# Mixture of experts: three experts in f32r and five in float32 column tiles, where six and two stood

## The chip, the cores and the metric

The program runs on one core of a Trainium2 chip. The metric is the time of one execution on the device, in microseconds (us); the lower the better. One profiled execution gives the trace.

## What is computed

The reference is a two-layer block of a diffusion transformer on 256 latent and 256 context tokens of width 1024. Layer 0 mixes by Hyena convolutions and attention and has a dense feed-forward part, layer 1 mixes by an S5 scan and has a mixture of eight experts, of which each latent token takes two. Only the mixture of experts is touched:

```python
logits = (t @ router).astype(F32)                 # t: 256 x 1024
top_val, top_idx = lax.top_k(logits, TOP_K)       # TOP_K = 2 of 8
top_w = jax.nn.softmax(top_val, axis=-1)
gates = jnp.sum(jax.nn.one_hot(top_idx, N_EXPERTS, dtype=F32) * top_w[..., None], axis=1)
for e in range(N_EXPERTS):
    he = jax.nn.silu(t @ w_gate[e]) * (t @ w_up[e])   # 1024 x 3584 each
    out = out + gates[:, e:e + 1].astype(t.dtype) * (he @ w_down[e])   # 3584 x 1024
```

## The kernel before

The layers before the mixture take up the first half of the span and stay as they are. Then the router's logits are ranked per token (`route_tile`), which gives each chosen token its place in the expert's list (`posm`) and the number of tokens of each expert (`cnt`). An expert computes only the tokens that chose it: a matrix `Sel` of ones and zeros (places against tokens) gathers them with matmuls (`gather`), and its transpose scatters the results back into `acc` (`scatter`).

**Slots.** Experts 0 and 1 have the slots 0 and 1. `route_order` sorts the other six by count; the slots 2 to 7 get their numbers as registers of SP (`nc.values_load`), so the loads of these experts' weights (`eload`) are issued at an address that SP reads only then. Slots 0 to 5 have 128 places each. The last two, `PAIR` and `PAIR + 1`, have 64 places each and share one tile of 128.

**Two ways to multiply.** The weights come as tiles of 1 MB (128 x 2048 float32, `kload`, `eload`), from a ring of raw tiles (`w`, `x1w`, `zw`: 8 in the steady part); an expert has 42 of them. Slots 0 to 5 (`up_big`, `down_big`) use f32r: `wsplit` splits each tile into a high and a low part on ACT (L196) and DVE (L197), and `mm3` issues three matmuls (L186 to L188) on each block of 128x512 weights. The pair (`up_pair`, `down_pair`) multiplies the raw tile in float32, with no split: an expert's 64 places are 64 columns of TensorE's array, and the two experts' matmuls write the lower and the upper 64 partitions of the same bank (L1844, L1887).

**Order.** The columns of 3584 are cut into `NP = 4` pieces of 1024, 1024, 1024 and 512. A task is a slot and a piece: its gate and up products, then, one task later, its down product. The tasks of the pair stand at the places 2, 8, 14 and 20 of the list. SP issues the loads in this order; ACT, DVE and PE have their instructions from the recording layer's scheduler, and each engine works its list in order. At the end `finish`, `scatter` and a norm follow. If an expert has more tokens than places, a second path (`overflow_expert`) computes the rest; it stands behind a branch on the largest excess.

Of the kernel before, what the change touches and what calls it, by code (L numbers as in the profile page):

```python
# [17 lines left out]
P = 128  # L18
# [10 lines left out]
def build(tc, A, out, stages=("s0", "mix0", "ffn0", "mix1", "moe"), dbg=None):  # L29
# [1127 lines left out]
    R_, rr = {}, {}  # L1157

# [17 lines left out]
    def route_setup(mp, tp, hf):  # L1176

        hfS = hp.tile([P, 2, 2, D], F32R, tag="hH", name="hfS")
        R_.update(tp=tp, hf=hf, hfH=hfS[:, 0], hfL=hfS[:, 1])
        for nm in ("lg", "rk", "sel", "gate", "posm"):  # L1180
            R_[nm] = mp.tile([P, 2, NE], F32, name=nm)
        R_["cnt"] = mp.tile([P, NE], F32, name="cnt")
        R_["tie"] = mp.tile([P, NE, NE], F32, name="tie")
        S.dma_start(R_["tie"].rearrange("p a b -> p (a b)"), A["k_tie"])

    def route_tile(t, x_):
# [42 lines left out]
        rr[t] = r  # L1229
# [9 lines left out]
    def route_slots(tp, e2):  # L1239

        Sel = tp.tile([P, 2, 2, P], F32R, tag="Sel", name="Sel", bufs=1)
# [5 lines left out]
    def place(t, s):  # L1247
        return R_["posm"][:, t, s:s + 1] if s < 2 else R_["posS"][:, t, s - 2:s - 1]

    def gate_of(t, s):  # L1250
        return R_["gate"][:, t, s:s + 1] if s < 2 else R_["gateS"][:, t, s - 2:s - 1]

    def route_gates(tp, m2):
# [3 lines left out]
        v = [m2.tile([P, 2, 1], F32, name="v%d" % i, bufs=1) for i in range(2)]  # L1257
# [18 lines left out]
    def route_order(tp, m2):  # L1276


        n = NE - 2
        cnt, posm, gate = R_["cnt"], R_["posm"], R_["gate"]  # L1280
        sh = [P, n, n]

        def scr(nm):
            return m2.tile([P, n, n], F32, name="or" + nm, tag="or" + nm, bufs=1)
        a, q = scr("H"), scr("L")
        co = cnt[:, 2:].unsqueeze(1).to_broadcast(sh)
        ce = cnt[:, 2:].unsqueeze(2).to_broadcast(sh)
        V.tensor_tensor(q, co, ce, op=OP.is_equal)
        V.tensor_tensor(a, co, ce, op=OP.is_gt)
        V.tensor_tensor(q, q, R_["tie"][:, 2:, 2:], op=OP.mult)  # L1290
# [13 lines left out]
        R_["gateS"] = tp.tile([P, 2, n], F32, name="gateS")  # L1304
        num = tp.tile([P, n], F32, name="onum")
        numi = tp.tile([P, n], I32, name="onumi")
        by_place(num, iota[:, 1:1 + n])
        V.tensor_copy(numi, num)
        for t in range(2):
            by_place(R_["posS"][:, t, :], posm[:, t, 2:])  # L1310
            by_place(R_["gateS"][:, t, :], gate[:, t, 2:])
        cap = R_["cap"] = tp.tile([P, NE], F32, name="ocap")
        G.memset(cap[:, 0:2], float(P))
        V.tensor_scalar(cap[:, 2:], rank, float(n - 2) - 0.5, -64.0, OP.is_gt, OP.mult)
        V.tensor_scalar(cap[:, 2:], cap[:, 2:], float(P), None, OP.add)
# [3 lines left out]
    def route_scatter(SelT, Sel):  # L1319

        b = fbank("selT")
        for e in range(2):
            for t in range(2):
                o = e * 256 + t * P
                T.transpose(b[:, o:o + P], Sel[:, t, e, :].bitcast(F32), ident)
        S.activation(SelT, b.rearrange("p (e t) -> p e t", e=2), AF.Copy)
# [18 lines left out]
    def moe_first(sp, w0=()):  # L1345
# [6 lines left out]
        ws = [kload(A["od_moe_w_gate"][0, 0], 2 * u, 0, 1024) for u in range(2)]  # L1352
# [291 lines left out]
    def overflow_expert(ei, rnd, op_, hq, m2, dP, hfH, hfL, acc, Wg, Wu, Wd, NC):  # L1644
# [11 lines left out]
        xg = m2.tile([P, KD, 256], F32, tag="xgL", name="xg2", bufs=1)  # L1656
# [41 lines left out]
        y = hq.tile([P, D], F32, tag="hL", name="oy")  # L1698
# [10 lines left out]
    if "moe" in stages:  # L1709
# [27 lines left out]
        if True:  # L1737
            m2 = open_pool(es4, "moe2", 2)

            def gather(e2):  # L1740

                if e2 % 2:
                    xB = hq.tile([P, 2, KD, 256], F32R, tag="hL", name="xB")
                    xH, xL = xB[:, 0], xB[:, 1]
                else:
                    xH = m2.tile([P, KD, 256], F32R, tag="xgH", name="xgH", bufs=1)
                    xL = m2.tile([P, KD, 256], F32R, tag="xgL", name="xgL", bufs=1)
                Sel = route_slots(mp, e2)
                for k2 in range(KD // 2):
                    b = bank("xg", "yb") if e2 == 0 and k2 % 2 else fbank("xg")  # L1750
                    u = hd_tile()
                    for k in range(2):
                        kc = (k2 * 2 + k) * P
                        cs = slice(k * 256, (k + 1) * 256)
                        for i, (src, t) in enumerate(((hfH, 0), (hfH, 1), (hfL, 0), (hfL, 1))):
                            T.matmul(b[:, cs], src[:, t, kc:kc + P], Sel[:, t].rearrange("p e s -> p (e s)"),
                                     start=(i == 0), stop=(i == 3))
                    for k in range(2):
                        cs = slice(k * 256, (k + 1) * 256)
                        modulate(u[:, cs], b[:, cs], k2 * 2 + k, k)  # L1760
                    ks = slice(k2 * 2, k2 * 2 + 2)
                    u = u.rearrange("p (k s) -> p k s", k=2)
                    S.activation(xH[:, ks, :], u, AF.Copy)
                    V.tensor_tensor(xL[:, ks, :], u, xH[:, ks, :].bitcast(F32), op=OP.subtract)
                SelT[e2] = m2.tile([P, 2, 256], F32R, tag="SelT", name="SelT", bufs=2)
                route_scatter(SelT[e2], Sel)
                return xH, xL

            def gather_pair():

                Sel = mp.tile([P, 2, P], F32R, tag="Sel", name="SelP", bufs=1)
                for t in range(2):
                    for i in range(2):
                        V.tensor_scalar(Sel[:, t, 64 * i:64 * i + 64], iota[:, 0:64], place(t, PAIR + i), None,
                                        OP.is_equal)
                xP = m2.tile([P, KD, P], F32, name="xP", bufs=1)
                for k4 in range(2):
                    b = fbank("xp")
                    for k in range(4):
                        kc = (k4 * 4 + k) * P  # L1780
                        for i, (src, t) in enumerate(((hfH, 0), (hfH, 1), (hfL, 0), (hfL, 1))):
                            T.matmul(b[:, k * P:(k + 1) * P], src[:, t, kc:kc + P], Sel[:, t, :],
                                     start=(i == 0), stop=(i == 3))
                    for k in range(4):
                        modulate(xP[:, k4 * 4 + k, :], b[:, k * P:(k + 1) * P], k4 * 4 + k, k % 2)
                b = fbank("selP")
                for t in range(2):
                    T.transpose(b[:, t * P:(t + 1) * P], Sel[:, t, :].bitcast(F32), ident)
                for t in range(2):
                    T.matmul(b[:, 256:258], Sel[:, t, :].bitcast(F32),  # L1790
                             R_["gateS"][:, t, PAIR - 2:PAIR], start=(t == 0), stop=(t == 1))
                SelT[PAIR] = m2.tile([P, 256], F32R, name="SelTP", bufs=1)
                S.activation(SelT[PAIR], b[:, 0:256], AF.Copy)
                gp = m2.tile([P, 1], F32, name="gp", bufs=1)
                V.tensor_copy(gp[0:64], b[0:64, 256:257])
                V.tensor_copy(gp[64:128], b[64:128, 257:258])
                return xP, gp

            NP = 4
# [5 lines left out]
            def hidden(bs):  # L1805

                hds_ = []
                for g, u in zip(*bs):
                    hd = hd_tile()
                    S.activation(hd, g, AF.Silu)  # L1810
                    V.tensor_tensor(hd, u, hd, op=OP.mult)
                    hds_.append(hd)
                return hds_

            def up_big(s, c, xH, xL, so):
                o, w = piece(c)
                nh, nk = w // 512, 2048 // w
                bs = []
                for i, W in enumerate((Wg, Wu)):
                    bb = [bank("mgu", "gu", 4) for _ in range(nh)]  # L1820
                    for u in range(KD // nk):
                        get = first.pop((s, c, i, u), None) or wsplit(eload(W, num[s], nk * u, o, w))
                        for h in range(nh):
                            for kk in range(nk):
                                k = nk * u + kk
                                mm3(bb[h], xH[:, k, so:so + P], xL[:, k, so:so + P],
                                    *get(kk * w + h * 512, 512), k == 0, k == KD - 1)
                    bs.append(bb)
                return hidden(bs)

            def up_pair(c, xP):
                o, w = piece(c)
                nh, nk = w // 512, 2048 // w
                bs = []
                for W in (Wg, Wu):
                    bb = [bank("pgu", "gu", 4) for _ in range(nh)]
                    for u in range(KD // nk):
                        ws = [eload(W, num[PAIR + i], nk * u, o, w) for i in range(2)]
# [250 lines left out]
```

## Time and profile before

| | |
|---|---|
| median of 3 runs | 2019.73 us (2016.52 to 2019.82) |
| the profiled execution | 2018.54 us |
| its span, first to last instruction | 2016.8 us |
| mean granted clock of TensorE | 0.969 |
| PE busy | 1860.4 us (92%) |
| DVE, ACT busy | 1394.2, 1037.2 us |
| DMA queue of the weights (q1) | 514.73 MB, 68.2% of 16 engines |

The page's first part gives each engine's busy time, its second cuts the span into 40 slices. A stretch's own limit is read from tables of stretches (busy time of each engine, granted clock, share and rate of the DMA engines) and from the instructions in order of time. The expert stage runs from about 1041 us to 1997 us.

### The profile page before, as it was taken

The page shows a single profiled execution, that of the slowest core. Times are in us where ns is not written, and L with a number is a line of the kernel's source. Part 1 is how long each engine was busy: PE and PEld are TensorE (multiplying, and loading weights), DVE is VectorE, ACT ScalarE, POOL GpSimd, SP SyncE. Part 2 cuts the span into 40 slices and gives each one's busy share as a digit, 9 for nine tenths or more (in the row PEclk, how much of TensorE's full clock was granted, in tenths as well). Part 3 has the DMA queues.
Part 4 walks back from the last instruction along what each step waited for, and adds up shares of the span by engine and source line. Part 5 has one row for each costly group of instructions (what it writes and reads, how often), then busy time and mean ns, then how long its engine had stood idle before and what let it go on. Part 6 is the DMA issues. An engine that isn't in the chain of part 4 may idle for free. (4 is left out here: it accounts for less than half of the span.)

```text
span 2016.8 us, 25616 instructions
## 1 busy us (share of the span) xinstructions
PE 1860.4 (92%) x9278; PEld 1369.1 (68%) x9278; DVE 1394.2 (69%) x2054; ACT 1037.2 (51%) x1492; POOL 160.2 (8%) x144
## 2 busy tenths in 40 slices
PE   5999999989999999865879999999999999999996
PEld 2667667867777787655658467846785687567775
DVE  6575775688875476486778358935883588578886
ACT  3522355543333365325466347724772477457765
POOL 1000310001111001055220000000000000000000
PEclk9999999989999999887979999999999999999998
DMA  9474314436666656637557999899999999999992
GB/s 350 162 261 149 134 42 176 160 112 212 219 209 201 221 188 245 233 121 272 211 223 261 368 409 397 332 356 410 405 368 378 413 384 360 340 385 352 355 336 109
DMA packets 196970, 545.55 MB, mean 271 GB/s; under 512 B 32620, under 2 KB 62421, under 8 KB 189285
## 3 DMA queue, kind: packets, MB, share of 16 engines
q1 hardware_dynamic: 165884, 514.73, 68.2%
q10 hardware_dynamic: 29400, 23.50, 4.0%
q0 software_dynamic: 1552, 5.62, 1.0%
q8 instruction: 75, 1.23, 0.2%
q14 instruction: 59, 0.48, 0.1%
HBM read 517.85 MB, written 25.89 MB: 270 GB/s over the span
## 5 line engine op out<-in xcount | busy, mean ns | idle before, releaser
L197 DVE TENSOR_TENSOR wl<-w,wh 128x1024 fp32r<-128x1024 f32 x380 | 449.7, 1224 | 101.7 <-ACT wh L196 98.9
L196 ACT ACTIVATE wh<-w 128x1024 fp32r<-128x1024 f32 x390 | 395.4, 1055 | 190.8 <-PE dn L187 49.0
L186 PE MATMUL mgu<-wh,xgH 128*128 128x512 f32 x448 | 178.4, 399 | 0.0
L187 PE MATMUL mgu<-wh,xgL 128*128 128x512 f32 x448 | 176.8, 396 | 0.0
L188 PE MATMUL mgu<-wl,xgH 128*128 128x512 f32 x448 | 168.4, 399 | 0.9 <-DVE wl L197 0.7
L196 ACT ACTIVATE wh<-zw 128x1024 fp32r<-128x1024 f32 x122 | 124.3, 1057 | 53.5 <-DMA zw<-in_od_moe_w_down_dram 29.3
L197 DVE TENSOR_TENSOR wl<-x1w,wh 128x1024 fp32r<-128x1024 f32 x122 | 142.9, 1218 | 11.4 <-ACT wh L196 11.0
L186 PE MATMUL gu<-hH,wh 128*128 128x512 f32 (+1 forms) x384 | 146.9, 383 | 2.2 <-ACT hH L196 2.2
L197 DVE TENSOR_TENSOR wl<-zw,wh 128x1024 fp32r<-128x1024 f32 x122 | 142.4, 1218 | 7.9 <-ACT wh L196 7.6
L188 PE MATMUL gu<-hL,wh 128*128 128x512 f32 (+1 forms) x384 | 145.2, 379 | 0.0
L187 PE MATMUL gu<-hH,wl 128*128 128x512 f32 (+1 forms) x384 | 144.3, 376 | 0.0
L196 ACT ACTIVATE wh<-x1w 128x1024 fp32r<-128x1024 f32 x124 | 126.0, 1056 | 19.6 <-PE yb L187 6.9
L186 PE MATMUL yb<-wh,mdH 128*128 128x512 f32 x336 | 133.5, 398 | 0.7 <-ACT mdH L196 0.7
L187 PE MATMUL yb<-wh,mdL 128*128 128x512 f32 x336 | 132.4, 394 | 0.0
L188 PE MATMUL yb<-wl,mdH 128*128 128x512 f32 x336 | 116.0, 400 | 11.6 <-DVE wl L197 11.6
L188 PEld LDWEIGHTS mgu<-wl,xgH 128*128 128x128 f32 x448 | 84.5, 189 | 23.8 <-DVE wl L197 4.1
L186 PEld LDWEIGHTS mgu<-wh,xgH 128*128 128x128 f32 x448 | 84.7, 189 | 20.0 <-ACT wh L196 1.0
L187 PEld LDWEIGHTS mgu<-wh,xgL 128*128 128x128 f32 x448 | 84.7, 189 | 18.9
L186 PE MATMUL mgu<-wh,xB 128*128 128x512 f32 x224 | 88.2, 394 | 2.0 <-ACT wh L196 2.0
L186 PEld LDWEIGHTS gu<-hH,wh 128*128 128x128 f32 x384 | 73.6, 192 | 20.2 <-issue 5.9
L187 PE MATMUL mgu<-wh,xB 128*128 128x512 f32 x224 | 87.1, 392 | 0.0
L188 PE MATMUL mgu<-wl,xB 128*128 128x512 f32 x224 | 82.7, 394 | 0.1
(722 smaller groups left out, 3775.1 us busy)
## 6 DMA issues: line engine op xcount, KB each, us to landing
w<-in_od_moe_w_up_dram SPq DMA_DIRECT2D x56, 1024.0 KB
w<-in_od_moe_w_gate_dram SPq DMA_DIRECT2D x55, 1024.0 KB
w<-in_od_moe_w_down_dram SPq DMA_DIRECT2D x54, 1024.0 KB
w<-in_ada_w_dram SPq DMA_DIRECT2D x48, 1024.0 KB
zw<-in_od_moe_w_down_dram SPq DMA_DIRECT2D x31, 1024.0 KB
x1w<-in_od_moe_w_up_dram SPq DMA_DIRECT2D x29, 1024.0 KB
x1w<-in_od_moe_w_gate_dram SPq DMA_DIRECT2D x28, 1024.0 KB
x1w<-in_od_moe_w_down_dram SPq DMA_DIRECT2D x27, 1024.0 KB
```

The costliest lines, as they stand in the source:

```text
L186: T.matmul(b, aH, bH, start=start, stop=False)
L187: T.matmul(b, aL, bH, start=False, stop=False)
L188: T.matmul(b, aH, bL, start=False, stop=stop)
L196: S.activation(h, src, AF.Copy)
L197: (eng or V).tensor_tensor(l, src, h.bitcast(F32), op=OP.subtract)
```

## The change

Only expert 1 (`ST = 1`) keeps a fixed slot, slot 0. The other seven are sorted by count. Slots 1 and 2 have 128 places and use f32r, as slot 0 does. Slots 3, 4 and 5 form the set T with 96, 96 and 64 places, which fill two tiles of 128: tile 0 holds 64 places of slot 5 and 64 of slot 4, tile 1 holds 64 and 32 places of slot 3 and 32 of slot 4. Slots 6 and 7 are the set P, 64 places each in one tile, as the pair was. Both sets multiply in float32 (`set_up`, `set_down`): per block of weights one matmul for each piece of a tile, so five in T (64, 64, 64, 32 and 32 columns wide) on the blocks of three experts and two in P.

So three experts are multiplied in f32r where there were six, and five in float32 where there were two. The sets' work is cut into steps (`set_gate`, `set_hidden`, `set_down`, for each piece), T's twelve first, then P's; `mid` runs after each gate, up and down product of an f32r expert and takes steps so that the tiles of the sets keep in proportion to the tiles of the f32r experts (`seen`). Two more raw tiles (`fw`) join the ring after the third gather.

```diff
+    ST = 1
...
+    def place(t, s):
+        return R_["posm"][:, t, ST:ST + 1] if s == 0 else R_["posS"][:, t, s - 1:s]
+
+    def route_slots(tp, groups, n):
+
+        Sel = tp.tile([P, 2, n], F32R, tag="Sel", name="Sel", bufs=1)
         for t in range(2):
-            for e in range(2):
-                V.tensor_scalar(Sel[:, t, e, :], iota, place(t, e2 * 2 + e), None, OP.is_equal)
+            for s, p0, c0, w in groups:
+                V.tensor_scalar(Sel[:, t, c0:c0 + w], iota[:, p0:p0 + w], place(t, s), None, OP.is_equal)
         return Sel
...
+        c1 = scr("H")[:, 0]
+        c2 = scr("L")[:, 0]
+        V.tensor_scalar(c1, rank, 1.5, -32.0, OP.is_gt, OP.mult)
+        V.tensor_scalar(c2, rank, 3.5, -32.0, OP.is_gt, OP.mult)
+        V.scalar_tensor_tensor(c1, c1, float(P), c2, OP.add, OP.add)
+        G.memset(cap, float(P))
+        V.tensor_copy(cap[:, ST + 1:], c1[:, 0:m])
+        V.tensor_copy(cap[:, 0:ST], c1[:, m:])
...
-        ws = [kload(A["od_moe_w_gate"][0, 0], 2 * u, 0, 1024) for u in range(2)]
+        ws = [kload(A["od_moe_w_gate"][0, ST], 2 * u, 0, 1024) for u in range(2)]
...
+            NP = 4
+
+            SETS = {"T": ((3, 4, 5), (((2, 5, 0, 0, 64), (1, 4, 0, 64, 64)),
+                                      ((0, 3, 0, 0, 64), (0, 3, 64, 64, 32), (1, 4, 64, 96, 32)))),
+                    "P": ((6, 7), (((0, 6, 0, 0, 64), (1, 7, 0, 64, 64)),))}
+            num, gs_, xs_, SelT = [ST], {}, {}, {}
...
+            def gather_set(w):
+
+                tiles = SETS[w][1]
+                n = len(tiles)
+                Sel = route_slots(mp, [(s, p0, i * P + c0, m) for i, g in enumerate(tiles) for _, s, p0, c0, m in g],
+                                  n * P)
+                x = m2.tile([P, KD, n * P], F32, name="x" + w, bufs=1)
+
+                def put(k0, nb, b):
+                    for k in range(nb):
+                        modulate(x[:, k0 + k, :], b[:, k * n * P:(k + 1) * n * P], k0 + k, k % 2)
+                dispatch(Sel, n * P, put)
...
+            def up_big(s, c, mid):
...
+                                mm3(bb[h], xH[:, k, :], xL[:, k, :], *get(kk * w + h * 512, 512), k == 0, k == KD - 1)
+                    for h in range(nh):
+                        if i == 0:
+                            hds_.append(hd_tile())
+                            S.activation(hds_[h], bb[h], AF.Silu)
+                        else:
+                            V.tensor_tensor(hds_[h], bb[h], hds_[h], op=OP.mult)
+                    mid(units(c))
+                return hds_
...
+            def set_up(w, c, W):
+
+                o, wd = piece(c)
+                nh, nk = wd // 512, 2048 // wd
+                es_, tiles = SETS[w]
+                bb = [bank("sgu", "gu", 4) for _ in range(len(tiles) * nh)]
+                for u in range(KD // nk):
+                    ws = [eload(W, num[e], nk * u, o, wd) for e in es_]
+                    for kk in range(nk):
+                        k = nk * u + kk
+                        for h in range(nh):
+                            for i, g in enumerate(tiles):
+                                for wi, _, _, c0, m in g:
+                                    T.matmul(bb[i * nh + h][c0:c0 + m], xs_[w][:, k, i * P + c0:i * P + c0 + m],
+                                             ws[wi][:, kk * wd + h * 512:kk * wd + h * 512 + 512],
                                              start=(k == 0), stop=(k == KD - 1))
+                return bb
...
+            def set_gate(w, c):
+                for j, b in enumerate(set_up(w, c, Wg)):
+                    S.activation(hdS[j], b, AF.Silu)
+
+            def set_hidden(w, c):
+                bb = set_up(w, c, Wu)
+                for j, b in enumerate(bb):
+                    V.tensor_tensor(hdS[j], b, hdS[j], op=OP.mult)
+                for j in range(len(bb)):
+                    b = bank("sht", "mt", 1)
+                    for f in range(4):
+                        T.transpose(b[:, f * P:(f + 1) * P], hdS[j][:, f * P:(f + 1) * P], ident)
+                    S.activation(hdS[j], b, AF.Copy)
+
+            def set_down(w, c):
+                o, wd = piece(c)
+                nh = wd // 512
+                es_, tiles = SETS[w]
+                n = len(tiles)
+                bb = [bank("sy", "gu", 4) for _ in range(n * 2)]
+                for u in range(wd // 256):
+                    ws = [eload(Wd, num[e], o // P + 2 * u, 0, 1024) for e in es_]
+                    for f2 in range(2):
+                        f = 2 * u + f2
+                        for h in range(2):
+                            for i, g in enumerate(tiles):
+                                for wi, _, _, c0, m in g:
+                                    a = (f % 4) * P + c0
+                                    T.matmul(bb[h * n + i][c0:c0 + m], hdS[i * nh + f // 4][:, a:a + m],
+                                             ws[wi][:, f2 * 1024 + h * 512:f2 * 1024 + (h + 1) * 512],
+                                             start=(f == 0), stop=(f == wd // P - 1))
+                for h in range(2):
+                    for i in range(n):
+                        y = yS[:, i, h * 512:(h + 1) * 512]
+                        if c:
+                            V.tensor_tensor(y, bb[h * n + i], y, op=OP.add)
+                        else:
+                            S.activation(y, bb[h * n + i], AF.Copy)
+                if c == NP - 1:
+                    for i in range(n):
+                        done.append((w, i))
...
+            tasks = [(s, c) for s in range(3) for c in range(NP)] + [None]
+            steps = [(f, w, c) for w in "TP" for c in range(NP) for f in (set_gate, set_hidden, set_down)]
+            done, ybs = [], {}
+            all_b, all_s, seen = 3 * 42, 5 * 42, {"big": 0, "small": 0}
+
+            def mid(n):
+
+                seen["big"] += n
+                for d in done:
+                    scatter(*finish(*d))
+                done.clear()
+                while steps and i and seen["small"] * (all_b - 18) <= (seen["big"] - 10) * all_s:
+                    f, w, c = steps.pop(0)
+                    f(w, c)
+                    seen["small"] += units(c, len(SETS[w][0]))
...
-            tasks = [(s, c) for s in range(PAIR) for c in range(NP)]
-            for c, i in zip(range(NP), (2, 8, 14, 20)):
-                tasks.insert(i, (PAIR, c))
...
+                    hd_ = up_big(s, c, mid)
...
+                    if task is not None:
+                        mid(units(c1))
+                pend = (task, turn(hd_)) if task is not None else None
...
+                    hdS = [m2.tile([P, 512], F32, name="hdS%d" % j, bufs=1) for j in range(4)]
+                    num += route_order(mp, hdS)
+                    gather_set("T")
+                    xy = hq.tile([P, 2, 2048], F32R, tag="hL", name="xy")
+                    yS = mp.tile([P, 2, D], F32, tag="y", name="yS")
+                    gather(1, [xy[:, 1, h * 1024:(h + 1) * 1024].rearrange("p (k s) -> p k s", k=KD) for h in range(2)])
+                if i == 2:
+                    gather_set("P")
+                if task == (1, 0):
+                    gather(2)
+                    fw = hp.tile([P, 2, 2048], F32, tag="hH", name="fw")
+                    late = more_raw(fw[:, 0], fw[:, 1])
```

On PE the rows of the sets replace those of the pair. Before, in the pair's gate product, all matmuls are 64 wide (`pgu` is the bank, `zw`, `x1w` and `w` are raw tiles, `xP` the gathered tokens):

```order
L1844 MATMUL pgu<-w,xP 64x512
L1844 MATMUL pgu<-x1w,xP 64x512
L1844 MATMUL pgu<-w,xP 64x512
L1844 MATMUL pgu<-x1w,xP 64x512
L1844 MATMUL pgu<-w,xP 64x512
```

Now, at the beginning of T's first gate step (`sgu` is the bank, `x1w` and `sp` raw tiles, `xT` the tokens of both tiles):

```order
L1872 MATMUL sgu<-x1w,xT 64x512 x2
L1872 MATMUL sgu<-sp,xT 64x512
L1872 MATMUL sgu<-sp,xT 32x512
L1872 MATMUL sgu<-x1w,xT 32x512
L1872 MATMUL sgu<-x1w,xT 64x512 x2
L1872 MATMUL sgu<-sp,xT 64x512
L1872 MATMUL sgu<-sp,xT 32x512
L1872 MATMUL sgu<-x1w,xT 32x512
```

Five rows' matmuls come back for each of the 168 blocks: three of 64 columns, two of 32. In some steps the scheduler pulls the pieces of tile 1 ahead of those of tile 0: over all of T's steps the 32-wide ones stand as 182 pairs or singles instead of 168.

On SP the loads that need the experts' numbers stand behind `TENSOR_LOAD onumi`. Before, eight static loads stand between the second `zw` of expert 0 and the numbers:

```order
L153 DMA zw<-in_od_moe_w_gate_dram 128x2x1024 x2
L153 DMA sp<-in_od_moe_w_up_dram 128x2x1024
L153 DMA x1w<-in_od_moe_w_up_dram 128x2x1024 x2
L153 DMA w<-in_od_moe_w_up_dram 128x2x1024
L153 DMA w<-in_od_moe_w_down_dram 128x2x1024 x3
L153 DMA zw<-in_od_moe_w_down_dram 128x2x1024
L1316 TENSOR_LOAD onumi
```

Now the numbers come right after it, seven of them, and then T's first tiles:

```order
L153 DMA zw<-in_od_moe_w_gate_dram 128x2x1024 x2
L1334 TENSOR_LOAD onumi
L1334 ISA x2
L1334 TENSOR_LOAD onumi
L1334 ISA x2
```

With the four gate and four up tiles of the first piece, 12 static tiles are issued ahead of the numbers where 20 were.

## Rows read from the trace of the kernel before

**Rows 1.** The page, part 2: busy tenths of PE and DMA in 40 slices.

```profile
PE   5999999989999999865879999999999999999996
...
DMA  9474314436666656637557999899999999999992
```

**Rows 2.** Stretches: busy us of the engines, granted clock, DMA share, GB/s.

```profile
809.60:811.40 1.80, 1.80 (x8) 0.16 (x8) 1.62 (x4) 1.25 (x2) 0.00 (x0) 0.50 0.90 378
...
1020.00:1040.00 20.00, 8.58 (x57) 6.09 (x58) 15.92 (x44) 10.51 (x20) 6.90 (x5) 0.55 0.38 153
...
1336.00:1358.00 22.00, 20.57 (x91) 7.51 (x88) 0.00 (x0) 1.28 (x3) 0.00 (x0) 1.00 1.02 414
1410.00:1450.00 40.00, 39.09 (x173) 31.40 (x172) 35.31 (x36) 29.71 (x35) 0.00 (x0) 1.00 1.03 413
...
1890.00:1930.00 40.00, 39.32 (x173) 31.20 (x172) 37.50 (x39) 28.36 (x32) 0.00 (x0) 1.00 0.89 324
```

**Rows 3.** Order of time, PE, first f32r task: start us, us, engine, line, operation.

```profile
1046.94 0.62 PE L186 MATMUL mgu<-wh,xgH 128*128 128x512 f32 x2
...
1050.15 0.40 PE L186 MATMUL mgu<-wh,xgH 128*128 128x512 f32 x1
...
1068.29 0.40 PE L186 MATMUL mgu<-wh,xgH 128*128 128x512 f32 x1
```

**Rows 4.** Order of time, PE, within a pair chunk.

```profile
1342.30 0.59 PE L1844 MATMUL pgu<-zw,xP 128*64 128x512 f32 x1
1342.36 0.59 PE L1844 MATMUL pgu<-w,xP 128*64 128x512 f32 x1
1342.73 0.59 PE L1844 MATMUL pgu<-zw,xP 128*64 128x512 f32 x1
```

**Rows 5.** Order of time, PE, a group of transposes and the next matmul.

```profile
1969.32 0.60 PE L1857 MATMUL mht<-cpk,hd 128*128 128x128 f32 x4
1969.67 0.47 PE L187 MATMUL mgu<-wh,xgL 128*128 128x512 f32 x1
```

**Rows 6.** Order of time, PE, eight passes 32 wide, what follows, and eight at another clock.

```profile
102.52 1.06 PE L237 MATMUL adp<-w,scol 128*32 128x512 f32 x8
103.51 0.50 PE L186 MATMUL tm<-wh,hH 128*128 128x512 f32 x1
...
809.56 1.93 PE L237 MATMUL adp<-w,scol 128*32 128x512 f32 x8
```

**Rows 7.** Order of time, PE, from 64 wide to 32 wide.

```profile
225.11 1.08 PE L1005 MATMUL pv<-PT,vt 128*64 128x256 f32 x4
226.12 1.49 PE L237 MATMUL adp<-w,scol 128*32 128x512 f32 x12
```

**Rows 8.** Order of time, PE, the first pass of a pair chunk and its next.

```profile
1109.21 0.64 PE L1844 MATMUL pgu<-zw,xP 128*64 128x512 f32 x1
...
1109.69 0.59 PE L1844 MATMUL pgu<-zw,xP 128*64 128x512 f32 x1
```

**Rows 9.** Order of time, DVE and SP: counts, experts' numbers, first dynamic load.

```profile
1070.73 0.16 DVE L1274 COPY cnt<-cnt 128x8 f32<-128x8 f32 x1
...
1082.22 0.16 DVE L1308 CAST onumi<-onum 128x6 int32<-128x6 f32 x1
...
1086.31 0.40 SPq L163 DMA_DIRECT2D zw<-in_od_moe_w_gate_dram  x1
```

**Rows 10.** A stretch of the expert stage, columns as in rows 2.

```profile
1090.00:1970.00 880.00, 856.38 (x3750) 610.17 (x3749) 618.66 (x617) 520.79 (x583) 0.00 (x0) 1.00 0.97 374
```

**Rows 11.** Order of time, ACT, around a pair chunk's end.

```profile
1341.64 0.60 ACT L1810 ACTIVATE hd<-pgu 128x512 f32<-128x512 f32 x1 [12.42 <-PE pgu L1844]
...
1357.91 2.00 ACT L196 ACTIVATE wh<-w 128x1024 fp32r<-128x1024 f32 x2 [14.82 <-DMA w<-in_od_moe_w_down_dram]
```

**Rows 12.** Order of time, PE, the last down product.

```profile
1996.77 0.40 PE L188 MATMUL yb<-wl,mdH 128*128 128x512 f32 x1
```

More of the change, by code (lines that the diff above doesn't have):

```diff
@@ L1256, in route_gates @@
         m = [tp.tile([P, 2, NE], F32, name="m%d" % i) for i in range(2)]
-        v = [m2.tile([P, 2, 1], F32, name="v%d" % i, bufs=1) for i in range(2)]
+        v2 = m2.tile([P, 2, 2, 1], F32, name="v2", bufs=1)
+        v = [v2[:, i] for i in range(2)]
         tq = tp.tile([P, 2, NE], F32, name="tq")
@@ L1769, in gather_pair @@
[L1769 to L1797, printed above, removed]
@@ L1799, in build, with dispatch @@
-            NP = 4
+            NP = 4
[3 more added lines that the diff above has]
+            num, gs_, xs_, SelT = [ST], {}, {}, {}
+            gts = m2.tile([P, 4], F32, name="gts", bufs=1)
+            def dispatch(Sel, n, put):
+                nb = 512 // n
+                for k0 in range(0, KD, nb):
+                    b = fbank("xg")
+                    for k in range(nb):
+                        kc = (k0 + k) * P
+                        for i, (src, t) in enumerate(((hfH, 0), (hfH, 1), (hfL, 0), (hfL, 1))):
+                            T.matmul(b[:, k * n:(k + 1) * n], src[:, t, kc:kc + P], Sel[:, t, :],
+                                     start=(i == 0), stop=(i == 3))
+                    put(k0, nb, b)
@@ new lines, in gather @@
+            def gather(s, at=None):
+                if at is None:
+                    xH = m2.tile([P, KD, P], F32R, tag="xgH", name="xgH", bufs=1)
+                    xL = m2.tile([P, KD, P], F32R, tag="xgL", name="xgL", bufs=1)
+                else:
+                    xH, xL = at
+                Sel = route_slots(mp, ((s, 0, 0, P),), P)
+                def put(k0, nb, b):
+                    u = hd_tile()
+                    for k in range(nb):
+                        modulate(u[:, k * P:(k + 1) * P], b[:, k * P:(k + 1) * P], k0 + k, k % 2)
+                    u = u.rearrange("p (k s) -> p k s", k=nb)
+                    S.activation(xH[:, k0:k0 + nb, :], u, AF.Copy)
+                    V.tensor_tensor(xL[:, k0:k0 + nb, :], u, xH[:, k0:k0 + nb, :].bitcast(F32), op=OP.subtract)
+                dispatch(Sel, P, put)
+                SelT[s], = route_scatter(m2, Sel, 1, "b", 2)
+                xs_[s] = xH, xL
@@ L1854, in turn @@
+            def turn(hds_):
+                dH, dL = [m2.tile([P, 1024], F32R, tag="md" + n, name="md" + n, bufs=1) for n in "HL"]
                 for j, hd in enumerate(hds_):
@@ L1991, in build @@
                         SY.dma_start(dP[r].rearrange("e p c -> p e c"), pk)
+                    hfS = hp.tile([P, 2, 2, D], F32R, tag="hH", name="hfO")
+                    hfH, hfL = hfS[:, 0], hfS[:, 1]
+                    for t in range(2):
+                        for h in range(2):
+                            cs = slice(h * 512, (h + 1) * 512)
+                            u = hd_tile()
+                            S.activation(u, xr[:, t, cs], AF.Copy, scale=rr[t])
+                            split_to(hfH[:, t, cs], hfL[:, t, cs], u)
                     for r in range(2):
@@ L1994, in build @@
                             overflow_expert(ei, r, op_, hq, m2, dP, hfH, hfL, acc, Wg, Wu, Wd, FFE // 512)
-            sqrt_table(done[2][:, D - 1:D].bitcast(F32))
-            scatter(acc, *done)
+            sqrt_table(done[3][:, D - 1:D].bitcast(F32))
+            scatter(*done, last=True)
             ptags = ["mdL", "mdH"]
```

241 lines of the change are left out of this document (85 added, 156 removed).

## The prediction

> **What bounds the kernel now.** First I read the page's 40 slices [rows 1]: from slice 23 on PE stands at 9 and the DMA engines at 8 or 9, so the expert stage (about 1041 to 1997 us) is nearly full on two resources at once. A table of stretches says which ends last [rows 2]. Where one float32 pair chunk runs (1336 to 1358), the transfers move 414 GB/s, and PE is busy 20.6 of 22 us: it waits for tiles. From 1410 to 1450 they still move 413 GB/s, although by then PE runs f32r experts without a gap; they fill the buffers that the chunk had emptied. From 1890 to 1930 PE has no gap and the transfers fall to 324 GB/s. So over its length the stage is PE's, with a margin of some ten per cent, and a change is priced in PE's time, with the transfers as a floor.
>
> The unit is one weight block of 128x512. An f32r expert spends three matmuls on it: between the last two L186 of [rows 3] lie 26 triples in 18.14 us, so 0.698 us a block. An expert has 168 blocks (3584 x 1024 x 3 weights): 117 us, while its 42 tiles of 1 MB take 42 x 1.049 MB / 414 GB/s = 106 us. A float32 matmul leaves two records, which I call passes. In the pair [rows 4] the two experts' passes stand 0.06 us apart and each comes back after 0.43 us: both blocks cost 0.86 us, that is 0.43 a block and 72 us an expert.
>
> **What the change takes away.** Three experts leave the f32r path: 3 x 168 x 0.698 = **-351.8 us**. The pair stays as it is (set P). Transposes: 21 groups of four go, 14 come with set T; a group delays PE by 0.35 us [rows 5]: -2.5. One scatter fewer is 8 matmuls of 0.23: -1.9. The gathers issue a little less; I put them at nothing.
>
> **What set T costs.** The three experts are in two tiles of places. Per block of each expert the order issues five float32 matmuls: A and B, 64 wide, side by side (tile 0); C, 64 wide, in the columns of A, then D and E, 32 wide, at 64 and 96 (tile 1). Do C, D and E run together? The trace of before holds no such mix, but it holds the parts. Four 32-wide matmuls do run together: eight passes take 1.06 us [rows 6]. And one place goes from 64 wide to 32 wide: pv, then adp [rows 7]. The four passes of pv overlap each other (1.08 us in all, in one half of the columns). The first 32-wide pass starts at 226.12, 0.07 us before the end of the last 64-wide one (225.11 + 1.08 = 226.19). The same 0.07 stands from 32 wide to 128 wide (102.52 + 1.06 = 103.58, next start 103.51 [rows 6]). I read it so: matmuls of one width overlap, and a new width starts when the old has nearly drained.
>
> So A, B and C, then D and E, alternate. A run of 64 wide has two passes of A beside B and two of C; the first lasts 0.48 until the next start [rows 8], two follow at 0.43, the last is waited out (0.59 - 0.07 = 0.52): 1.86. The run of 32 wide: 0.45 (the 1.06 of [rows 6] less the last pass) + 0.52 = 0.97. Together 2.83 us a group, where 1.72 would do if all ran together. 168 groups make 475; in the built order 14 of the 32-wide pairs are torn apart, each another slot of 0.97: **+489 us**. Bounds: without any loss at a change, three slots of 0.86, 433; with as many more torn pieces again and an extra fill each, 520. I take 489, because [rows 7] is the very change.
>
> The Trainium skill, page "TensorEngine Tiling (Array Packing)", section Key Properties, says that a change of the tiling mode, not of the tile, drains TensorE, and it lists 128x64 and 128x32 as two configurations. By that rule the five matmuls cost what I take, and the trace agrees in its one such place (0.07 us before the end).
>
> **The start of T.** SP issues 20 static tiles today before it must know the experts' numbers; then only 12. The numbers come from counts copied at 1070.73 and are cast at 1082.22, and the first dynamic tile goes out at 1086.31 [rows 9]; the six splits and small operations between stay, so I leave these times. PE has used up 12 tiles at 1047 [rows 3] + 12 x 4 x 0.698 = 1081. T needs three tiles, 7.6 us at 414 GB/s, and its gather, which needs the places. I set T's first matmul at 1096: 15 us, of which 7 are the gather's own work. While PE stood still half of the time before (1020 to 1040), the granted clock was 0.55 [rows 2], so some 4 us more run at the lower level: **+12**; bounds 0 and 25.
>
> **Transitions.** After each of the 24 set steps ACT and DVE, which work in order, empty the banks before they split the next f32r tile. After a gate step I count 2 us (three evacuations of 0.60, then a split of 1.00, some of it during the last matmuls [rows 11]), 0.5 to 1 after the others, where splits stand ahead: some 21 us. What they replace is PE's idle time in the stage, 23.6 us between 1090 and 1970 (880 less 856.4 [rows 10]), which now comes at the set steps instead of the pair's chunks. So 0; bounds -15 and +25.
>
> **Transfers.** In T's stretch (63 tiles f32r, 126 of T) PE has 176 + 489 + 50 = 715 us of work, the transfers 189 x 2.53 = 479: no bound, about 277 GB/s. In P's stretch (43 and 84) PE has 120 + 145 + 25 = 290, the transfers 321 less 8 to 10 tiles that lie ready: **+10**; bounds 0 and 25. From T's first tile to the last, 324 tiles take 820 us at least, which would end at 1906: far before PE.
>
> **Sum.** The profiled execution took 2018.5 us (span 2016.8), 1.2 below the median of the runs shown. 2018.5 - 351.8 - 2.5 - 1.9 + 489 + 12 + 0 + 10 = **2173 us**, 7.7% slower. The tail after the last yb (1996.77 [rows 12]), 20 us, is untouched.
>
> **Rivals.**
> 1. The widths share the array after all, so C, D and E overlap: T costs 168 x 1.72 = 289, 200 less: **1973 us**, 2.3% faster. For it: the columns do not collide, and four narrow matmuls overlap [rows 6]. Against: adp's matmuls in all four column groups started together, only when pv was nearly done, though pv held one half of the columns [rows 7]. The point from which it decides: below (489 - 154) / 168 = 2.0 us a group the change gains. Chance 0.08. The skill's same page, section Theoretical Speedup, gives up to 2x at 64 and 4x at 32 wide, which alone would lead here; no row shows the two mixed.
> 2. The granted clock sinks during T, because half of the array is idle and every group drains twice. Eight passes took 1.93 us where the granted clock was 0.50 (1.2 GHz) and 1.06 elsewhere [rows 2, 6]; T would cost some 890 instead of 489: about **2570**. Against it: through the pair's chunk, with PE waiting for tiles, the clock stays at 1.00 [rows 2]. Chance 0.03.
> 3. The change doesn't do what it says, because an expert has more tokens than places and the second path runs. One expert read again costs 42 x 2.53 = 106 us at least: from **2280** up. The reference's inputs send 36, 68, 77, 79, 34, 67, 89 and 62 tokens; expert 1 has 128 places, then 89 and 79 fit in 128, 77 and 67 in 96, 62 in 64. Chance 0.02.
> 4. DMA becomes the bound and interleaving wins the floor: 1906 plus 8 tiles of work and the tail, about **1950**. It needs rival 1 and no transition cost: chance 0.02.
>
> **How the numbers follow.** My case (2173) has 0.85. Its own range adds the bounds: low 2173 - 56 - 12 - 10 - 3 = 2092, high 2173 + 31 + 13 + 15 + 8 = 2240 (the transitions by a part of their bounds, as all ends seldom meet). The rest, 0.15, lies outside and may stay there, so the range is 2092 to 2240. Faster by over 0.2%, about what a measurement can tell from no change: rivals 1 and 4, 0.10. Within it: 0.02, when bounds and a part of rival 1 meet. Slower: 0.88.
>
> **What would show it.** Right: in the changed profile sgu and sy stand as 128*64 and 128*32 in turn, a 32-wide start 0.07 us before a 64-wide end, a group of five in about 2.8 us; T's stretch is some 715 us long with about 280 GB/s and clock 1.00; P's runs near 400 GB/s; the first sgu near 1096. Wrong: 32-wide passes that start within 0.1 us of a 64-wide one and a group in 1.7 us, which is rival 1; or passes of 1.06 us, which is rival 2. If T's groups take 2.8 us and the time is still under 2092, my price for the experts that left, or for PE's idle time, is wrong.

## The result and the profile after

The changed kernel takes **2195.51 us** (median of 4 runs, 2194.17 to 2196.06) against 2019.78 (2016.52 to 2021.29): a ratio of 1.087, 95% interval 1.085 to 1.089. Forecast were 2173 us, between 2092 and 2240. The profiled execution took 2196.06 us, its span is 2194.3. Of all executions named below one, of `t_32_64`, ran at a lower granted clock throughout (0.826 in the mean, 2189.19 us), and its comparison leaves it out.

The page's slices, the answer to [rows 1]:

```profile
PE   5999999899999989657899999999999999999996
...
DMA  9574126357666575457077676787677788999994
```

PE stands at 9 from its 22nd slice to the last but one. The transfers, at 8 or 9 before, are now at 6 to 8 for fourteen slices. The stretches of the expert stage (us, busy us of PE, PEld, DVE, ACT and POOL, granted clock, DMA share, GB/s), the answer to [rows 2, 10]:

```profile
1040.00:1050.00 10.00, 5.98 (x26) 5.76 (x27) 6.01 (x24) 3.41 (x6) 2.42 (x2) 0.50 0.00 0
1050.00:1060.00 10.00, 10.00 (x36) 8.30 (x37) 3.79 (x5) 4.21 (x7) 0.00 (x0) 0.64 0.00 0
...
1090.00:1100.00 10.00, 5.05 (x24) 4.06 (x24) 3.72 (x21) 2.07 (x4) 0.00 (x0) 0.73 0.56 211
1100.00:1110.00 10.00, 6.97 (x26) 5.51 (x28) 1.81 (x8) 1.22 (x3) 0.00 (x0) 0.50 1.03 418
1109.10:1831.50 722.40, 704.38 (x2661) 273.02 (x2660) 194.08 (x208) 166.84 (x204) 0.00 (x0) 1.00 0.74 279
1831.50:2156.00 324.50, 306.74 (x1286) 166.90 (x1286) 135.25 (x138) 109.51 (x127) 0.00 (x0) 0.99 1.02 407
```

T's stretch (fifth row) has PE busy for 704 of 722 us, the transfers at 279 GB/s and the clock at 1.00: PE's time is what it takes. P's stretch (sixth) runs at 407 GB/s. Ahead of them, around 1045 and 1105, PE is busy only 6 to 7 of 10 us, and its clock is at 0.50.

One unit of T, four groups of five matmuls, in order of time on PE (start us, us, line, operation, count). A row's form is that of its first record; 40 passes are 16 of A and B, 8 of C, 16 of D and E. The second row shows the last two of the 40 by themselves, from a closer window:

```profile
1185.59 11.44 PE L1872 MATMUL sgu<-w,xT 128*64 128x512 f32 x40
...
1196.43 0.60 PE L1872 MATMUL sgu<-w,xT 128*32 128x512 f32 x2
1196.96 0.64 PE L1872 MATMUL sgu<-x1w,xT 128*64 128x512 f32 x1
```

From 1185.59 to 1196.96 are 11.37 us, **2.84 us a group**, where 2.83 were forecast from [rows 4, 6, 7, 8]. The last two 32-wide passes end at 1196.43 + 0.60 = 1197.03, and the next 64-wide one starts 0.07 us earlier, as from pv to adp [rows 7]. The trace models the ends of matmuls; from start to start it is 0.53 us (1196.43 to 1196.96), where passes of one width follow each other after 0.43. T's twelve steps, each from its first pass to its last, add up to 498.3 us.

The start of T, in order of time on PE, DVE and SP, the answer to [rows 9]:

```profile
1042.46 0.15 DVE L1230 SCALAR_TENSOR_TENSOR posm<-pos,sel 128x8 f32<-128x8 f32 x1
...
1048.45 3.67 PE L1778 MATMUL xg<-Sel,hfS 128*128 128x128 f32 x16 [1.93 <-DVE hd L1354]
...
1051.92 0.73 PE L186 MATMUL mgu<-wh,xgH 128*128 128x512 f32 x1
...
1088.41 0.17 DVE L1321 CAST onumi<-onum 128x7 int32<-128x7 f32 x1
...
1093.07 0.40 SPq L163 DMA_DIRECT2D sp<-in_od_moe_w_gate_dram  x1
...
1100.03 2.08 PE L1778 MATMUL xg<-Sel,hfS 128*128 128x256 f32 x8 [1.24 <-DVE xT L1354]
...
1109.12 1.98 PE L1872 MATMUL sgu<-x1w,xT 128*64 128x512 f32 x4
```

The first mgu comes at 1051.92 (1046.94 before, [rows 3]), the numbers at 1088.41 (1082.22), the first dynamic load at 1093.07 (1086.31), and T's first matmul at 1109.12, not at 1096.

### The profile page after: what moved, and what is told of

It reads as the page before. It is cut to its first block, busy times and chain, and to the rows that moved or that the text cites. A ratio compares the mean times of both kernels' runs of the same rounds, so it can differ in the third digit from the quotient of the medians.

```text
span 2194.3 us, 25064 instructions
## 1 busy us (share of the span) xinstructions
PE 2015.8 (92%) x9448; PEld 1199.2 (55%) x9448; DVE 1093.7 (50%) x1799; ACT 779.0 (35%) x1228; POOL 160.0 (7%) x145
## 3 DMA queue, kind: packets, MB, share of 16 engines
q1 hardware_dynamic: 165884, 514.73, 62.3%
## 5 line engine op out<-in xcount | busy, mean ns | idle before, releaser
L197 DVE TENSOR_TENSOR wl<-w,wh 128x1024 fp32r<-128x1024 f32 x232 | 275.6, 1220 | 219.8 <-ACT wh L196 216.5
L196 ACT ACTIVATE wh<-w 128x1024 fp32r<-128x1024 f32 x242 | 246.4, 1054 | 200.6 <-PE dn L187 48.9
L1872 PE MATMUL sgu<-w,xT 128*32 128x512 f32 (+1 forms) x568 | 201.3, 607 | 0.0
L1905 PE MATMUL sy<-w,hdS 128*64 128x512 f32 (+1 forms) x392 | 140.3, 603 | 0.1
L1872 PE MATMUL sgu<-x1w,xT 128*64 128x512 f32 (+1 forms) x280 | 121.7, 620 | 0.0
L197 DVE TENSOR_TENSOR wl<-zw,wh 128x1024 fp32r<-128x1024 f32 x52 | 61.5, 1219 | 116.8 <-ACT wh L196 116.8
L186 PE MATMUL mgu<-wh,xgH 128*128 128x512 f32 x224 | 90.9, 406 | 5.2 <-ACT wh L196 5.1
L1872 PE MATMUL sgu<-zw,xT 128*64 128x512 f32 (+1 forms) x232 | 91.1, 605 | 0.0
L187 PE MATMUL mgu<-wh,xgL 128*128 128x512 f32 x224 | 89.4, 400 | 0.0
L188 PE MATMUL mgu<-wl,xgH 128*128 128x512 f32 x224 | 85.0, 403 | 3.0 <-DVE wl L197 2.8
```

The costliest lines, as they stand in the source:

```text
L186: T.matmul(b, aH, bH, start=start, stop=False)
L187: T.matmul(b, aL, bH, start=False, stop=False)
L188: T.matmul(b, aH, bL, start=False, stop=stop)
L196: S.activation(h, src, AF.Copy)
L197: (eng or V).tensor_tensor(l, src, h.bitcast(F32), op=OP.subtract)
L1872: T.matmul(bb[i * nh + h][c0:c0 + m], xs_[w][:, k, i * P + c0:i * P + c0 + m], ws[wi][:, kk * wd + h * 512:kk * wd + h * 512 + 512], start ...
```

## The experiments

The theory: a change of matmul width drains the array, and matmuls of two widths never share it. So C with D and E costs a slot and two changes in every group. The rivals: the third slot alone is the price; the changes alone are; narrow matmuls cost something of their own; or the time goes elsewhere.

### One width: all of T in 32-wide pieces (t_32)

```
-  for wi, _, _, c0, m in g:
+  for wi, c0, m in parts(w, i, g):   # for T: (wi, c, 32) for c in range(c0, c0 + m, 32)
```

The line changes in set_up and set_down.

> Set T with every piece cut into 32-wide ones: per group 8 matmuls of one width instead of five of two, same tiles, same transfers, same result. Theory (a change of width drains the array and the two widths never overlap): four column groups run side by side, a group takes 2 x 0.86 = 1.72 us, T's steps some 310 instead of 498 us, and the kernel 2195.5 - 188 = about 2007 us (2000 to 2025, as the transfers of T's stretch come near their bound). Rival 1 (a slot is a slot, width does not matter; eight matmuls are more work than five): over 2195. Rival 2 (the weight loads, 0.11 to 0.14 us each in the changed kernel at either width, run one after another): 16 x 0.11 to 0.14 = 1.8 to 2.2 us a group, 2020 to 2085 us.

Measured: **1997.9 us**, ratio to the kernel before 0.989 (0.987 to 0.991). Eight 32-wide matmuls a group instead of five of two widths, and 198 us less than the changed kernel, a little below the expected 2000 to 2025. Its passes in T, in order of time on PE:

```profile
1190.25 0.62 PE L1878 MATMUL sgu<-zw,xT 128*32 128x512 f32 x2
1190.29 0.60 PE L1878 MATMUL sgu<-w,xT 128*32 128x512 f32 x2
1190.68 0.62 PE L1878 MATMUL sgu<-zw,xT 128*32 128x512 f32 x2
1190.71 0.60 PE L1878 MATMUL sgu<-w,xT 128*32 128x512 f32 x2
```

Four passes start every 0.43 us, the rate at which two start when they are 64 wide [rows 4]; 16 passes make 1.72 a group. T's steps take 303.4 us. Both rivals fall: in this kernel the additional matmuls and weight loads cost nothing that can be seen.

### One width: all of T 64 wide (t_64)

```
-  ((0, 3, 0, 0, 64), (0, 3, 64, 64, 32), (1, 4, 64, 96, 32))
+  ((0, 3, 0, 0, 64), (1, 4, 64, 64, 64))
```

> T's tile 1 holds two 64-wide pieces, so all four matmuls of a group are 64 wide. This leaves out places 64 to 95 of the third-largest set member (slot 3), which are computed nowhere; slot 4 gets 32 places that it does not need. Theory: no change of width, group 1.72 us, about 2007 us (2000 to 2025), the same as all 32 wide. Rival (narrow matmuls have a price of their own, for loads or issue): this one comes out faster than the all-32 kernel by more than 10 us. If neither comes near 2007, the price of T is not in the widths at all.

Measured: 1996.98 us (1995.23 to 1997.19), ratio 0.989 (0.987 to 0.990); T's steps 301.8 us. It cannot be told from the kernel above, so the rival falls: at one width, narrow pieces cost no more than wide ones. (The kernel leaves out 32 places of slot 3, so it is no version to keep.)

### Two slots, but with changes of width (t_32_64, t_32_64b)

```
+  if w == "T" and i == 1:   # only tile 1 in 32-wide pieces
```

The condition stands in `parts`, which is otherwise that of `t_32`.

> Only tile 1 of T is cut into 32-wide pieces; tile 0 stays 64 wide. Two slots a group, and 200 changes between 64 and 32 wide in the built order instead of 328. Theory: two slots of 0.86 and 0.13 us for each change (in the changed kernel 2.84 - 2.58 = 0.26 us for two): 289 + 26 + 21 of waits = 336, so 2195.5 - 162 = about 2033 us. Rival 1 (the third slot is the whole price, a change is free): as all 32 wide, about 2007. Rival 2 (the changes are the whole price, 188 us / 328 = 0.57 us each): 2195.5 - 128 x 0.57 = about 2122.

Measured: **2038.7 us**, ratio 1.009 (1.008 to 1.011); the theory's number is 2033. Rival 1 (2007) and rival 2 (2122) both miss it. The kernel was run once more for its rows.

> The kernel with only tile 1 cut into 32-wide pieces once more, for its profile at the full granted clock. Theory: a run of four 64-wide passes is left with the last pass waited out, 0.07 us before its end, then eight 32-wide passes start; in groups with both changes in place 1.72 + 2 x 0.13 = 1.98 us, T's steps together about 336 us, 2038 us in all. Rival (a change costs nothing by itself): groups of 1.72.

Measured: 2037.19 us. Two groups, in order of time on PE:

```profile
1179.58 0.61 PE L1878 MATMUL sgu<-zw,xT 128*32 128x512 f32 x4
1180.13 0.64 PE L1878 MATMUL sgu<-x1w,xT 128*64 128x512 f32 x1
...
1182.13 0.64 PE L1878 MATMUL sgu<-x1w,xT 128*64 128x512 f32 x1
...
1184.14 0.64 PE L1878 MATMUL sgu<-x1w,xT 128*64 128x512 f32 x1
```

A group takes 2.00 us, so two changes cost 0.28 on top of 1.72: **0.14 us each**. T's steps take 340.3 us. Of the 41 us between this kernel and the all-32 one, 37 lie in T's steps, and not all of that is changes: T's steps have 204 of them in the trace, 29 us at 0.14. The rest fits slots that stay partly empty, since in some units the order cuts the 32-wide passes into runs that don't fill whole slots of four: about 11 more slots of 0.86. The last gate and up steps have no such run; their 15 changes take them from 13.94 us in the all-32 kernel to 16.11, again 0.14 each. Between the changed kernel and this one lie 157 us, 158 in T's steps; the third slot (168 x 0.86 = 144) and 128 further changes (18) make 162.

### The same matmuls, sorted by width (t_sorted)

```
+  for wide in (64, 32):
+      for kk in range(nk): ...
+          if m == wide: T.matmul(...)
```

> The same matmuls as in the changed kernel, but in each unit (four groups) all 64-wide ones come first, then all 32-wide ones: 76 changes between 64 and 32 wide instead of 328, the third slot stays. Theory: 252 x 0.13 = 33 us less, about 2162 us. Rival 1 (a change is free, only the third slot counts): 2195, no change. Rival 2 (the changes are the whole price, 0.57 us each): 2195.5 - 252 x 0.57 = about 2052.

Measured: 2146.96 us (2143.68 to 2149.3), ratio 1.063 (1.062 to 1.065): 48 us less than the changed kernel, where 33 were expected. One unit on PE:

```profile
1186.85 0.64 PE L1874 MATMUL sgu<-x1w,xT 128*64 128x512 f32 x1
...
1192.91 4.58 PE L1874 MATMUL sgu<-zw,xT 128*64 128x512 f32 x18
1197.42 0.64 PE L1874 MATMUL sgu<-x1w,xT 128*64 128x512 f32 x1
```

Four groups take 10.57 us, 2.64 each, as three slots of 0.86 a group and two changes a unit make it; the third slot stays. Rival 1 (2195) and rival 2 (2052) both miss. T's steps fall from 498.3 to 453.0, by 45. The 12 us beyond the expected 33 fit the pairs of D and E that the order tore apart in the changed kernel and that sorting puts together again. The prediction counted 14 of them in the built order; PE's rows show 12. A step with one takes 46.56 us, a step of the same size with none 45.56, so each costs 1.00 us.

### T's first step after 20 units instead of 12 (t_late)

```
-  seen["small"] * (all_b - 18) <= (seen["big"] - 10) * all_s
+  seen["small"] * (all_b - 26) <= (seen["big"] - 18) * all_s
```

> The changed kernel with T's first step after 20 units of the first expert instead of 12 (the 10 and the 18 of the rule become 18 and 26); T keeps its two widths. Theory (between the last matmul of the 12 units and T's first one PE stands or crawls for 19.4 us, since nothing is left to run beside the numbers and T's gather; its first step also loses 5 us): with eight units left to run there, most of that goes: 2195.5 - 18 = about 2178 us (2174 to 2184), and the transfers before the numbers are known grow from 12 tiles to 20. Rival (the gap only moves: what is gained at the start is given back in P's stretch, which the transfers bound): 2190 or more.

Measured: **2168.57 us**, ratio 1.074 (1.072 to 1.075): 27 us less than the changed kernel, and less than the expected 2174 to 2184. Around T's first matmul, on PE:

```profile
1115.21 0.40 PE L188 MATMUL yb<-wl,mdH 128*128 128x512 f32 x1
1115.53 1.08 PE L1872 MATMUL sgu<-x1w,xT 128*64 128x512 f32 x4
```

and two stretches of the same kernel:

```profile
1040.00:1080.00 40.00, 37.36 (x161) 31.64 (x162) 26.19 (x50) 24.34 (x31) 2.40 (x2) 0.81 0.50 184
1080.00:1120.00 40.00, 39.79 (x188) 29.62 (x186) 32.18 (x67) 22.28 (x27) 0.00 (x0) 1.00 0.65 237
```

PE goes from yb to sgu without a gap and keeps the clock at 1.00; from 1040 to 1080 the transfers run at 184 GB/s, where the changed kernel's stood still (0 to 1 GB/s). T's steps are 8.3 us shorter as well (490.0). Some 5 us of that have nothing to do with the start: the scheduler's order has 7 torn pairs here instead of 12, 1.00 us each. The first step takes 45.56 us instead of 51.45: it has no torn pair (2 before), doesn't start at half clock, and has no matmuls of a gather inside. The third, which now has them, takes 52.01 instead of 50.49. The rival falls: at 2190 or more nothing would have been gained.

### A bank of its own for the first gather's second block (t_gbank)

```
-  b = fbank("xg")
+  b = bank("xg", "yb") if not xs_ and k0 % (2 * nb) else fbank("xg")
```

> The changed kernel with the second block of the first expert's gather in a bank of its own instead of in the bank of the first. Theory: from the second posm on DVE to the first mgu there are 6.23 us before and 9.46 us after the change, because the second block waits for the first one's four evacuations; with its own bank 6 to 7 us, and the cast of the numbers as much earlier against that posm (45.96 us after it now, 43 then). Rival (the wait is for the four modulations of the first bank itself, which mgu needs anyway): 9 us or more as now.

```profile
1041.19 0.15 DVE L1230 SCALAR_TENSOR_TENSOR posm<-pos,sel 128x8 f32<-128x8 f32 x1
...
1048.54 0.78 PE L186 MATMUL mgu<-wh,xgH 128*128 128x512 f32 x1
...
1084.34 0.16 DVE L1321 CAST onumi<-onum 128x7 int32<-128x7 f32 x1
```

These are its rows on DVE and PE: 7.35 us from posm to the first mgu instead of 9.46 (6 to 7 were expected), and 43.15 instead of 45.96 to the numbers. So 2.8 of the 4.45 us by which the change delays the numbers against that posm (41.51 before) come from the single bank: the rival falls. The kernel took 2192.14 us in its one run; a difference of 3 us is about what one run can't tell.

### Together: a version that beats both kernels (t_32_late, t_32_late_g)

> All of T 32 wide, and T's first step after 20 units. Theory: the two gains add, 1997.9 - 18 = about 1980 us (1975 to 1988). Rival 1 (with 32-wide pieces the transfers bound T's stretch, so a gain at the start is waited out later): 1990 to 1998. A floor by the transfers: 316 dynamic tiles x 2.53 = 799 us from 1093, eight tiles of work and the tail, about 1935; so 1980 would still be PE's time.

Measured: **1969.49 us** (1967.25 to 1970.22), ratio to the kernel before **0.974** (0.973 to 0.976). The two gains add, and more than the expected 18 us: 28 less than with 32-wide pieces alone, so below 1975 to 1988. As here all of T has one width, no torn pairs are in it. With the second bank too:

> T 32 wide, T's first step after 20 units, and the second block of the first gather in a bank of its own. Theory: the first mgu comes 2 us earlier against the second posm (7.35 instead of 9.46 us), and the numbers 3 us earlier, so the transfers too: 1969.5 - 2 to 3 = about 1967 us. Rival (the stage after that absorbs it): 1969.5, no change that can be told.

Measured: **1965.81 us** (1964.33 to 1966.76), ratio 0.974 (0.972 to 0.975), beside its own runs of the kernel before (2017.81). The intervals of the two ratios overlap; the bank's gain isn't shown.

### Two attempts to get more (t_32_late26, t_32_late_gw)

> As the kernel with T 32 wide and its first step after 20 units, but after 28. Theory: the gap at the start is already covered by the 20, so nothing more comes: within 4 us of that kernel, about 1980. Rival (the transfers set the end, and more static tiles ahead of the numbers start them earlier): 8 tiles x 2.53 = up to 20 us less, about 1965. Against both: with fewer f32r units left beside T and P, their stretches lean more on the transfers, and it is slower by 5 to 15 us.

Measured: 1973.27 us, ratio 0.976 (0.975 to 0.978), 4 us more than with 20 units, and the ranges don't overlap: the start is covered, more static tiles ahead buy nothing, and the loss named as the third case is there, though under its 5 us.

```
-  seen["small"] += units(c, len(SETS[w][0]))
+  seen["small"] += units(c, len(SETS[w][0])) * (2 if w == "T" else 3)
-  all_b, all_s = 3 * 42, 5 * 42
+  all_b, all_s = 3 * 42, 12 * 42
```

> As the kernel with T 32 wide, a late start and the second bank, and each tile of P counts 1.5 times as much as one of T in the rule that interleaves the sets with f32r units: T ends after 66 f32r units instead of 76, so ten more units lie beside P. Theory: P's stretch is bound by the transfers (413 to 417 GB/s with PE idle), T's is not (351 to 378 GB/s), so f32r units are worth more beside P; ten units of PE work at 2.8 us move to where PE waits, and of the 30 us of unused transfer time in T's stretch a part is used: about 1957 us (1950 to 1963). Rival (PE's idle time in P's stretch comes from the steps' own evacuations, not from the transfers): no change, 1967.

Measured: 1967.87 us against 1965.81 of the kernel that it changes: nothing gained, and my number, 1957, was wrong. T's stretch, from its first matmul to P's, of the kernel t_32_late_g, then of this one:

```profile
1112.20:1607.40 495.20, 485.07 (x3601) 242.42 (x3600) 179.23 (x195) 155.12 (x192) 0.00 (x0) 1.00 0.97 387
```

```profile
1111.90:1587.30 475.40, 464.21 (x3497) 225.48 (x3496) 157.71 (x175) 137.86 (x173) 0.00 (x0) 1.00 0.97 387
```

P begins after 70 f32r units instead of 78, so eight have moved. The transfers run at 387 GB/s in both: with 32-wide pieces T's stretch is itself within 7% of the 414 GB/s of [rows 2], and eight f32r units fewer in it did not raise that. Nothing is gained, as the rival had it; that its cause is the steps' own evacuations, as the rival also says, isn't shown by this run. The sum had left out that a unit brings its tile along: 2.53 us of transfer beside 2.8 us of PE, so that where the transfers bound the stretch, moving eight units can win 2 us by estimate, and not 10.

## Why the prediction was right, and where it was short

**Right:** the side, the mechanism of T's price and most of the size. The step on which it rested, that D and E wait for C because the widths differ, was read from one place of the trace of before [rows 7] and priced from parts [rows 4, 6, 8]: 2.83 us a group forecast, 2.84 measured. The torn pairs, priced at 14 us, cost 12: 12 in the trace, 1.00 us each. The three experts that left the f32r path, the transposes and the scatter were priced at -356.2 us and measure -351.1 (below).

The Trainium skill, page "TensorEngine Tiling (Array Packing)", section Key Properties, says that changing the tiling mode drains TensorE. The trace agrees, and the runs add the price: 0.14 us a change, and 0.86 us for the slot that the two widths cannot share. Its section Theoretical Speedup, with up to four times at 32 wide, agrees with the four passes per 0.43 us of the all-32 kernel as soon as there is one width.

**Rival 1** (widths overlap, 1973) fell with the row at 1196.96, **rival 2** (the clock sinks) with the 1.00 of T's stretch, **rival 3** (second path) with the bytes of the weights' queue, 514.73 MB on both pages, where the second path would have read weights once more, **rival 4** (transfers bound) with the 279 GB/s there.

**Short by 22 us.** PE's rows from the first mgu to the last yb say where. Each instruction counts up to the next one's start; the last two lines are idle time and what stands outside of this stretch.

| | before | after | measured | forecast |
|---|---|---|---|---|
| f32r matmuls (mgu, yb) | 713.0 | 365.8 | -347.2 | -351.8 |
| transposes (mht, sht) | 23.2 | 19.4 | -3.8 | -2.5 |
| scatters (sct) | 12.9 | 12.8 | -0.1 | -1.9 |
| gathers (xg, xp, selT, selP, gS) | 13.0 | 24.4 | +11.4 | "at nothing" |
| the pair; T and P | 163.5 | 655.2 | +491.7 | +489 |
| PE idle | 24.3 | 44.7 | +20.4 | start +12, transitions 0, transfers +10 |
| first mgu later, tail after yb | | | +5.1 | 0 |

That is +177.5, the difference of the spans (2016.8 and 2194.3), where 155 were forecast. PE's busy time in the two stretches, and so its idle time (950.23 - 925.92 and 1122.65 - 1077.92), is that of these rows (PE alone, before, then after):

```profile
1046.94:1997.17 950.23, 925.92 (x4060) 1.00 0.93 357
1051.92:2174.57 1122.65, 1077.92 (x4229) 0.99 0.79 304
```

What was mis-sized, in the prediction's terms:

- *The gathers, "at nothing"*, are half of it. T's gather was priced as if it took the place of one before, but nothing else is left for PE while it runs: its blocks wait 1.24 us each for an evacuation, and the clock stands at 0.73, then 0.50, so its matmuls themselves take longer.
- *The start of T: +12* was 25, its upper bound: 1109.12 instead of 1096, with the gather's own price in it. The step that failed is "the six splits and small operations between stay, so I leave these times". The numbers came at 1088.41, not 1082.22. Of these 6.2 us 1.75 lie ahead of the second posm (1042.46 instead of 1040.71), 2.8 come from the first gather, which now evacuates both its blocks from one bank (t_gbank), and the rest is left to the additional small operations for seven slots, which weren't tried by themselves. Also, PE's 12 units ended at 1089.7 and not at 1081, as the first mgu came 5 us later and ran at a clock of 0.64. The late start shows what the place costs: 28 us in the kernel with T 32 wide.
- *T: +489* was 498.3. PE has no idle time inside any of T's steps, so these are not waits. Steps with nothing else in them take 45.56 us, and 22.82 for the last piece; nine and three of them make 478, and the torn pairs 12 more. Most of the other 8 us are two things. The first groups of the first and the fourth step ran at half clock, 1.2 to 1.3 us more each. And 27 matmuls of slot 1's gather, 128 wide, stand inside the first and the third step, three times in each; every time they cost 0.5 to 0.8 us with the change of width, 3.9 in all. One such place, 0.70 us from the first xg to the next sgu:

```profile
1141.95 0.77 PE L1778 MATMUL xg<-Sel,hfS 128*128 128x128 f32 x5
1142.65 3.65 PE L1872 MATMUL sgu<-zw,xT 128*64 128x512 f32 x16
```

- *Transitions 0 and transfers +10* were 12 together: PE's idle time from 1109.1 to 2156 is 722.4 - 704.4 + 324.5 - 306.7 = 35.8 us, against 23.6 [rows 10]. So these two held.

## What to carry to other kernels

Count slots by width: in every run here two matmuls shared the array only if they were equally wide, so cut a set of unequal tiles into pieces of the narrowest width; more, smaller matmuls were free here, and the same three experts went from 498 to 303 us. Count also what else the order puts between them, gathers and scatters. Where widths must be mixed, sort by width within what lies in the buffers, at 0.14 us a change. And when data-dependent work replaces static work, look at what is left to run while its numbers are made: eight more static units there were worth 28 us.

## What the runs showed of the hardware that was not expected

A scatter that the order puts inside a set step pays the change of width again, as the gather inside T's steps does. In the changed kernel, in a step of P, in order of time on PE:

```profile
1950.67 1.07 PE L1872 MATMUL sgu<-zw,xP 128*64 128x512 f32 x2
1951.68 0.50 PE L1962 MATMUL sct<-xy,SelTb 128*128 128x512 f32 x1
1952.11 1.07 PE L1872 MATMUL sgu<-zw,xP 128*64 128x512 f32 x2
1953.11 0.50 PE L1963 MATMUL sct<-xy,SelTb 128*128 128x512 f32 x1
```

One 128-wide matmul of the scatter splits the pair: a 64-wide matmul that would have had a partner runs alone, two passes take 1.07 us, and the scatter starts 0.06 us before their end. That step, with eight such matmuls inside, took 20.11 us, others of its size 14.0; in `t_late` the order puts no scatter into the same step, and it takes 14.01. So a scatter's matmul costs about 0.8 us there. I had put the scatters at their own 0.23 us a matmul.
